# Output gate of the attention branch: a factor on the rows of the output weights, or a factor on the finished sums

## The chip, the cores and the metric

The kernel runs on one core of one Trainium2 chip. The metric is the device time of one launch in microseconds (us). The engines are named as the profile names them: PE (matrix multiply), PEld (its weight loads), DVE (VectorE), ACT (ScalarE), POOL (GpSimd) and SP (the queue that issues most DMAs). A difference of 0.3 % of this kernel's time is 3.5 us.

## The reference

One transformer block on x of shape (1, 1024, 1024), in float32: a normalisation, an input projection, two mixers side by side (a gated linear recurrence, and differential attention with 4 heads), one output projection for both, and a mixture of 16 experts. The lines that matter here:

```python
mix = jnp.dot(jnp.concatenate([y_lru, y_att], axis=-1), w_out[l])
x = x + gate1 * mix
h2 = rms_norm(x, g_norm2[l]) * (1.0 + scale2) + shift2
x = x + gate2 * expert_choice_ffn(h2, w_router[l], w1[l], w3[l], w2[l])
```

`gate1`, `scale2`, `shift2` and `gate2` are rows of 1024 numbers, one for each output column, worked out earlier from the input c. Since `gate1` scales columns of the result, it may as well scale the columns of `w_out`.

## The kernel before, in words

The program has five stages: projections and recurrence (0 to about 313 us in the trace), the attention loop (to 467), the output projection with residual, norm and router (to 575), the choice of tokens (to about 610), and the experts (to the end).

**Attention loop.** 32 steps, one for each head and tile of 128 query rows, are pipelined over `g`. In each step PE forms scores (`sc`), DVE adds the bias and finds the maximum (L768), ACT takes exponentials (`p`), DVE combines the two softmaxes (L807), PE transposes the weights (`pw`, L814), ACT copies them out (`wt`) and PE multiplies with the values (`pv`, 16 matmuls a step). Every fourth step a finished sum is evacuated: ACT copies `pv` to `o` (`o_evac`), POOL squares it in two pieces (`osq`, L837), and two steps later DVE reduces the squares over a row (`hov`, L845, first instruction of `o_rstd`), a short chain on DVE and POOL makes the inverse root (L846 to L858), POOL scales `o` (L861), and PE transposes it (`po`, L869) for `yatt`. PE, DVE and ACT run in the order in which the code was written (`manual_schedule`, L907). POOL and SP are outside that list and are put in order by the scheduler. All engines work through their own instructions strictly in order.

**Weights for the next stage.** `load_wo(k)` is called in eight of the loop's steps. It loads 128 rows of `w_out` (`wo`, L877), multiplies them on POOL by `gate1` in four pieces of 256 columns (L886), lets ACT round them to the high part (`who`, `wx0o` or `wos` by k), and lets POOL form the low part as a difference, again in four pieces (`wlo`, `wx1o`, `wos`, L890). The row `gate1` is spread over all partitions by one DMA before the loop (L906).

**Output projection.** For each of 8 tiles of 128 tokens: ACT and POOL (DVE in the first two tiles) split `y` into `yh` and `yl` (L1015). PE adds up 24 matmuls for each half of 512 columns (`mix`). `add_x` (L1040) lets DVE add the residual `xr` to the sums, half by half, the result over `xr`. ACT squares it into `tmp` (name `h2` in the code) with a row sum. PE transposes it (`ph`, L1059), ACT copies it (`x1T`), and PE multiplies with the router weights (`pl`, `pk`), from which DVE and ACT make the affinities (`afd`, L1098) and PE turns them (`pq`, L1101). After the next tile's first `add_x`, DVE makes `tmp = x1 * rs * na` (L1109), POOL adds `shift2` to all 1024 columns at once (L1110), and a DMA stores `tmp` as row tile of `h2d`, from which the experts gather later. The last tile takes its columns as 512, 256 and 256 (`mix7b`, `mix7c`), and forms the product on POOL (L1052). All engines but POOL and SP are ordered by the scheduler by estimated times here, too.

Of the kernel before, what the change touches and what calls it, by code (L numbers as in the profile page):

```python
# [8 lines left out]
F32 = mybir.dt.float32  # L9
F32R = mybir.dt.float32r  # L10
BF16 = mybir.dt.bfloat16
I32 = mybir.dt.int32
AF = mybir.ActivationFunctionType
ALU = mybir.AluOpType
# [4 lines left out]
P = 128  # L19
# [3 lines left out]
NT = S // P  # L23
NCT = 4
NH = 4
NE = 16
# [14 lines left out]
OA = (5, 6, 7)  # L41
NL0 = 16
NL1 = 30
XO = ("yh0", "yl0", "xr2", "xr0", "yh1", "yl1", "tmp0", "xr1", "na2", "shift2", "tmp1")
KG = 3
KA = 3
PI = 3
# [35 lines left out]
def tile_block(ctx: ExitStack, tc, x, cols, w_mod, b_mod, w_in, wa, wx, lam_qk, relT, w_out, g2, w_router,  # L83
               w1, w3, w2, jbits, jfrac, out):
    nc = tc.nc
    V, A, G_, T, SY = nc.vector, nc.scalar, nc.gpsimd, nc.tensor, nc.sync
# [29 lines left out]
    modd = [dram.tile([1, 2048], F32, name=f"modd{i}") for i in range(2)]  # L116
# [174 lines left out]
    mps, pms = {}, {}  # L291
# [583 lines left out]
    def load_wo(k):  # L875
        r = raw_tile(f"wo{k}", [P, D])
        SY.dma_start(out=r, in_=w_out[k * P:(k + 1) * P, :])  # L877
        if k < 3:
            woh[k], wol[k] = (wo1.tile([P, D], F32R, tag=tg, bufs=b_, name=f"{tg}o{k}") for tg, b_ in (("wh", NWH), ("wl", 3)))
        elif k == 3:  # L880
            woh[k], wol[k] = (wo1.tile([P, D], F32R, tag=f"wx{j}", bufs=1, name=f"wx{j}o") for j in range(2))
        else:
            woh[k], wol[k] = qk_tile(f"wos{k}", F32R)
        for q in range(4):
            qs = slice(q * 256, q * 256 + 256)
            G_.tensor_tensor(out=r[:, qs], in0=r[:, qs], in1=gate1[:, qs], op=ALU.mult)  # L886
        act(woh[k], r)
        for q in range(4):
            qs = slice(q * 256, q * 256 + 256)
            G_.tensor_tensor(out=wol[k][:, qs], in0=r[:, qs], in1=woh[k][:, qs].bitcast(F32), op=ALU.subtract)  # L890
# [10 lines left out]
    for k in range(NCT):  # L901
        G_.tensor_copy(y0[:, 0, k, :], y_lru[k][:, 0:P])
        G_.tensor_tensor(out=y0[:, 1, k, :], in0=y_lru[k][:, 0:P], in1=y0[:, 0, k, :].bitcast(F32), op=ALU.subtract)
    gate1 = ap.tile([P, 1024], F32, name="gate1")
    src = modd[0][:, 0:1024]
    SY.dma_start(out=gate1, in_=bass.AP(tensor=src.tensor, offset=src.offset, ap=[[0, P], [1, 1024]]))  # L906
    with tc.manual_schedule(engines={mybir.EngineType.PE, mybir.EngineType.DVE, mybir.EngineType.Activation}):  # L907
        for g in range(NG + 2):
            hn, u = divmod(g, 8)
# [64 lines left out]
    def row_bc(name, src):  # L974
        t_ = x_big(name, 0)
        SY.dma_start(out=t_, in_=bass.AP(tensor=src.tensor, offset=src.offset, ap=[[0, P], [1, 1024]]))
        return t_
# [7 lines left out]
    wrA = xt_["wrA"]  # L985
    G_.memset(wrA, 0.0)
    G_.tensor_tensor(out=wrA[:, :, 0:NE], in0=wr2, in1=a2c.unsqueeze(2).to_broadcast([P, KT, NE]), op=ALU.mult)
    shift2 = row_bc("shift2", modd[0][:, 1024:2048])
    na2 = row_bc("na2", modd[1][:, 0:1024])
    g2r = row_bc("tmp1", g2)  # L990
# [28 lines left out]
    for t in range(NT):  # L1019
# [7 lines left out]
        x1 = xr  # L1027
# [9 lines left out]

        def add_x(n):
            ns = slice(cuts[n] * P, cuts[n + 1] * P)
            add = V.tensor_tensor(out=x1[:, ns], in0=pms[n], in1=xr[:, ns], op=ALU.add)  # L1040
            if n == 0 and h2_pend:
                h2_pend.pop()(add)
            if n == 1 and t == NT - 1:
                with tc.issue_after(add.ins):
                    V.tensor_scalar(out=x_big("yh0", NT).bitcast(BF16)[:, 0:SE], in0=aTh[:, 0:SE], scalar1=jb.bitcast(F32),
                                    scalar2=None, op0=ALU.is_ge, op1=ALU.add, accum_out=cnt7)
            if t == 0 and n == 0:
                o_out(7)
            act(h2[:, ns] if t < NT - 1 else junk_[:, 0:(cuts[n + 1] - cuts[n]) * P], x1[:, ns], AF.Square, scale=1.0 / 32,
                accum_out=ssq2[:, t, n:n + 1])  # L1050
            if t == NT - 1:
                G_.tensor_tensor(out=h2[:, ns], in0=x1[:, ns], in1=na2[:, ns], op=ALU.mult)  # L1052
# [53 lines left out]
        if t < NT - 1:  # L1106
            def h2_fin(add, t=t, x1=x1, h2=h2):
                with tc.issue_after(add.ins):
                    V.scalar_tensor_tensor(out=h2, in0=x1, scalar=rs2[:, t:t + 1], in1=na2, op0=ALU.mult, op1=ALU.mult)  # L1109
                G_.tensor_tensor(out=h2, in0=shift2, in1=h2, op=ALU.add)  # L1110
                (G_ if t in HG else SY).dma_start(out=h2d[t * P:(t + 1) * P, :], in_=h2)

            h2_pend.append(h2_fin)
        else:
            with tc.issue_after(i_exp.ins):
                act(h2, h2, AF.Copy, scale=rs2[:, t:t + 1])
            i_h2 = G_.tensor_tensor(out=h2, in0=shift2, in1=h2, op=ALU.add)
            A.dma_start(out=h2d[sl, :], in_=h2)
# [31 lines left out]
        return lambda: V.tensor_scalar(out=o, in0=a, scalar1=b, scalar2=c, op0=ALU.mult, op1=ALU.add)  # L1150

    NR = 5
    rhs = late.tile([P, NT, NE, NR], BF16, name="rhs")
    tidx = late.tile([P, 56], F32, name="tidx")[:, 0:NT]
    pidx = late.tile([P, 1], F32, name="pidx")
    G_.iota(tidx, pattern=[[P, NT]], base=0, channel_multiplier=0, allow_small_or_imprecise_dtypes=True)
    G_.iota(pidx, pattern=[[0, 1]], base=0, channel_multiplier=1, allow_small_or_imprecise_dtypes=True)
    G_.tensor_copy(rhs[:, :, :, 0], tidx.unsqueeze(2).to_broadcast([P, NT, NE]))
# [8 lines left out]
    G_.tensor_copy(selb, bone.rearrange("p (e j) -> p e j", j=8)[:, :, 0])  # L1167
    idx = const.tile([P, NE], I32, name="idx")
    gat = const.tile([P, NE], F32, name="gat")
    slot = late.tile([P, NE, NT], F32, name="slot")  # L1170
    gth = []

    def pick(e, oh, pi):
# [290 lines left out]
```

## Time and profile before

| | |
|---|---|
| median of 3 runs | 1180.84 us (1180.72 to 1183.39) |
| the profiled execution itself | 1183.49 us |
| its span in the trace | 1181.8 us |
| mean granted clock of PE | 0.977 |
| PE busy | 1116.1 us (94 %) |
| DVE, ACT, POOL busy | 955.8, 791.3, 481.7 us |

The profiled execution is 2.65 us (0.22 %) above the median of the other runs, and its span is 1.7 us shorter than its own time. In rows of the timeline the columns are: start, duration, engine, line, operation, tiles, count, and in brackets the idle time ahead of it with what ended it. A row for one line lists minimum, median and maximum of one instruction in ns. A row for a stretch lists its bounds, its length, busy time of PE, PEld, DVE, ACT and POOL (with counts), the granted clock, the share of the DMA engines and GB/s.

### The profile page before, as it was taken

The numbers are of one execution on the slowest core, as the hardware profiler recorded it, in microseconds if no ns is written. First come the engines' busy times: TensorE is split into PE (matmuls) and PEld (weight loads), VectorE is DVE, ScalarE is ACT, GpSimd is POOL, SyncE is SP. The second block draws the span as 40 slices with busy tenths as digits, with TensorE's granted clock in tenths as the row PEclk, the third lists the DMA queues.
The fourth block names the chain that finished last, engine by engine and source line by source line (L and its number), as shares of the span: only waits on it lengthen the run. The fifth ranks groups of instructions, "written<-read, shape, count | busy, mean of one in ns | idle before, by whom it ended". The sixth has DMA issues, their size and how long they took to land.

```text
span 1181.8 us, 17872 instructions
## 1 busy us (share of the span) xinstructions
PE 1116.1 (94%) x6320; PEld 937.7 (79%) x6320; DVE 955.8 (81%) x1242; ACT 791.3 (67%) x1046; POOL 481.7 (41%) x540
## 2 busy tenths in 40 slices
PE   6999899999979999999569999999999999999996
PEld 4698898798869899777447888888888888888885
DVE  6897657875569896543679999999999999999995
ACT  7548282295467787543328887878888787888784
POOL 4693132133086646344534324444323444332400
PEclk9999999999999999999769999999999999999999
DMA  9765625704781505425799999999999999999911
GB/s 334 228 198 177 220 84 170 242 18 112 193 242 45 150 19 180 162 107 211 266 342 330 363 386 380 390 391 402 378 394 393 369 392 410 394 394 386 393 37 18
DMA packets 146994, 304.34 MB, mean 258 GB/s; under 512 B 16973, under 2 KB 43725, under 8 KB 146901
## 3 DMA queue, kind: packets, MB, share of 16 engines
q1 hardware_dynamic: 135008, 279.99, 65.7%
q0 software_dynamic: 5488, 19.45, 6.4%
q10 hardware_dynamic: 6408, 3.77, 1.1%
q8 instruction: 50, 0.82, 0.3%
q14 instruction: 40, 0.32, 0.1%
HBM read 277.95 MB, written 25.21 MB: 257 GB/s over the span
## 4 chain that ended last, share of the span: by engine, by line
PE 75%; DVE 7%; issue 5%; POOL 5%; DMA 5%; ACT 2%; SPq 1%; POOLq 0%; ACTq 0%; DVEq 0%
PE ab L93 28%; PE y L93 13%; PE mix L93 7%; PE pjz L93 4%; PE pjk L93 3%; PE sc L93 3%; PE pjv L93 3%; PE pv L93 3%; PE pw L814 2%; DMA wr<-in_w_mod_dram 2%; POOL wo L886 2%; PE pg L93 1%; DVE macc L623 1%; DMA wo<-in_w_out_dram 1%; PE pf L1348 1%
## 5 line engine op out<-in xcount | busy, mean ns | idle before, releaser
L1248 POOL TENSOR_SCALAR oh<-iot,slot 128x128 bf16<-128x128 bf16 x120 | 146.4, 1234 | 252.5 <-PE pf L1348 252.4
L93 PE MATMUL ab<-wh,xeh 128*128 128x512 f32 x512 | 202.2, 395 | 0.2 <-ACT xeh L90 0.2
L93 PE MATMUL ab<-wh,xel 128*128 128x512 f32 x512 | 199.7, 390 | 0.0
L93 PE MATMUL ab<-wl,xeh 128*128 128x512 f32 x512 | 157.7, 389 | 0.0
L93 PEld LDWEIGHTS ab<-wl,xeh 128*128 128x128 f32 x512 | 96.1, 188 | 20.4
L93 PEld LDWEIGHTS ab<-wh,xel 128*128 128x128 f32 x512 | 96.2, 188 | 19.5 <-DVE xel L1261 0.5
L93 PEld LDWEIGHTS ab<-wh,xeh 128*128 128x128 f32 x512 | 96.1, 188 | 19.5 <-ACT xeh L90 0.5
L141 DVE TENSOR_TENSOR wl<-w_0r,wh 128x1024 fp32r<-128x1024 f32 x79 | 96.8, 1226 | 10.2 <-ACT wh L90 0.4
L90 ACT ACTIVATE wh<-w_0r 128x1024 fp32r<-128x1024 f32 x81 | 86.1, 1062 | 24.8 <-PE ab L93 14.9
L141 DVE TENSOR_TENSOR wl<-w_3r,wh 128x1024 fp32r<-128x1024 f32 x79 | 96.7, 1225 | 6.2
L90 ACT ACTIVATE wh<-w_1r 128x1024 fp32r<-128x1024 f32 x79 | 83.5, 1058 | 23.7 <-PE ab L93 18.9
L90 ACT ACTIVATE wh<-w_3r 128x1024 fp32r<-128x1024 f32 x79 | 83.9, 1062 | 22.0 <-PE ab L93 17.4
L141 DVE TENSOR_TENSOR wl<-w_2r,wh 128x1024 fp32r<-128x1024 f32 x80 | 96.4, 1221 | 2.6 <-ACT wh L90 1.4
L90 ACT ACTIVATE wh<-w_2r 128x1024 fp32r<-128x1024 f32 x80 | 84.7, 1060 | 19.1 <-PE ab L93 18.7
L141 DVE TENSOR_TENSOR wl<-w_1r,wh 128x1024 fp32r<-128x1024 f32 x78 | 92.7, 1220 | 3.9 <-ACT wh L90 2.1
L768 DVE CUSTOM_DVE_ANT_0 p<-sc,bias 128x1024 f32<-128x1024 f32 x64 | 77.7, 1216 | 10.0 <-PE sc L93 9.9
L93 PE MATMUL y<-wh,htl 128*128 128x512 f32 x256 | 82.9, 395 | 0.0
L93 PE MATMUL y<-wh,hth 128*128 128x512 f32 x256 | 80.9, 396 | 0.0
L93 PE MATMUL y<-wl,hth 128*128 128x512 f32 x256 | 79.6, 391 | 0.0
L90 ACT ACTIVATE p<-p,stat 128x1024 f32<-128x1024 f32 x60 | 68.5, 1151 | 9.1 <-DVE stat L768 9.1
L93 PEld LDWEIGHTS pv<-v,wt 128*128 128x128 f32 x512 | 61.7, 192 | 2.5
L93 PE MATMUL pv<-v,wt 128*128 128x128 f32 x512 | 62.1, 275 | 0.0
(459 smaller groups left out, 2862.5 us busy)
## 6 DMA issues: line engine op xcount, KB each, us to landing
w_0r<-in_w_dram SPq DMA_DIRECT2D x81, 512.0 KB, 8.8
w_1r<-in_w_dram SPq DMA_DIRECT2D x79, 512.0 KB, 8.3
w_2r<-in_w_dram SPq DMA_DIRECT2D x78, 512.0 KB, 8.8
w_3r<-in_w_dram SPq DMA_DIRECT2D x77, 512.0 KB, 8.9
wr<-in_w_mod_dram SPq DMA_DIRECT2D x32, 512.0 KB, 4.9
wi<-in_w_in_dram SPq DMA_DIRECT2D x18, 512.0 KB, 4.4
w_5r<-in_w_dram SPq DMA_DIRECT2D x17, 512.0 KB, 8.0
wm<-in_w_mod_dram SPq DMA_DIRECT2D x32, 256.0 KB, 4.8
```

Source lines behind the costliest of these rows:

```text
L90: return A.activation(out=out, in_=in_, func=func, **kw)
L93: return T.matmul(out, lhsT=lhsT, rhs=rhs, start=start, stop=stop)
L141: return (eng or V).tensor_tensor(out=lo, in0=src, in1=hi.bitcast(F32), op=ALU.subtract)
L623: V.scalar_tensor_tensor(out=macc[i], in0=w, scalar=sc[:, k:k + 1], in1=macc[i], op0=ALU.mult, op1=ALU.add)
L768: V.tensor_tensor_reduce(out=p_, in0=scp[g, j], in1=prs[h][0][:, b0:b0 + S], op0=ALU.add, op1=ALU.min, scale=1.0, scalar=3.0e38, accum_out ...
L814: T.transpose(pw[:, b * P:(b + 1) * P], pt_[g, 0][:, kt * P:(kt + 1) * P], ident)
L886: G_.tensor_tensor(out=r[:, qs], in0=r[:, qs], in1=gate1[:, qs], op=ALU.mult)
L1248: G_.tensor_scalar(out=oh[:, t, :], in0=iot, scalar1=slot[:, e, t:t + 1], scalar2=None, op0=ALU.is_equal)
L1348: T.transpose(pt[:, b * P:(b + 1) * P], sa[:, b * P:(b + 1) * P], ident)
```

## The change

The weights are no longer multiplied by `gate1`; the sums are. In `load_wo` the four products of each call are left out, and ACT and POOL split the plain rows. In `add_x`, DVE first multiplies the sums in PSUM by `gate1` into `tmp` and then adds `xr` in a second instruction, whose inputs both lie in SBUF. The row `gate1` is loaded at the start of the output projection, ahead of `shift2`. POOL's addition of `shift2` is cut into four pieces of 256 columns (tiles 0 to 6). Four small tiles (`rhs`, `tidx`, `pidx`, `slot`) move to another pool, which opens after the output projection.

```diff
-XO = ("yh0", "yl0", "xr2", "xr0", "yh1", "yl1", "tmp0", "xr1", "na2", "shift2", "tmp1")
+XO = ("gate1", "yh0", "yl0", "xr2", "xr0", "yh1", "yl1", "tmp0", "xr1", "na2", "shift2", "tmp1")
...
-        for q in range(4):
-            qs = slice(q * 256, q * 256 + 256)
-            G_.tensor_tensor(out=r[:, qs], in0=r[:, qs], in1=gate1[:, qs], op=ALU.mult)
         act(woh[k], r)
...
-    gate1 = ap.tile([P, 1024], F32, name="gate1")
-    src = modd[0][:, 0:1024]
-    SY.dma_start(out=gate1, in_=bass.AP(tensor=src.tensor, offset=src.offset, ap=[[0, P], [1, 1024]]))
...
+    gate1 = row_bc("gate1", modd[0][:, 0:1024])
     shift2 = row_bc("shift2", modd[0][:, 1024:2048])
...
-            add = V.tensor_tensor(out=x1[:, ns], in0=pms[n], in1=xr[:, ns], op=ALU.add)
+            V.tensor_tensor(out=h2[:, ns], in0=pms[n], in1=gate1[:, ns], op=ALU.mult)
+            add = V.tensor_tensor(out=x1[:, ns], in0=h2[:, ns], in1=xr[:, ns], op=ALU.add)
...
-                G_.tensor_tensor(out=h2, in0=shift2, in1=h2, op=ALU.add)
+                for q in range(4):
+                    qs = slice(q * 256, q * 256 + 256)
+                    G_.tensor_tensor(out=h2[:, qs], in0=shift2[:, qs], in1=h2[:, qs], op=ALU.add)
...
-    rhs = late.tile([P, NT, NE, NR], BF16, name="rhs")
-    tidx = late.tile([P, 56], F32, name="tidx")[:, 0:NT]
-    pidx = late.tile([P, 1], F32, name="pidx")
+    rhs = moe.tile([P, NT, NE, NR], BF16, name="rhs")
+    tidx = moe.tile([P, 56], F32, name="tidx")[:, 0:NT]
+    pidx = moe.tile([P, 1], F32, name="pidx")
...
-    slot = late.tile([P, NE, NT], F32, name="slot")
+    slot = moe.tile([P, NE, NT], F32, name="slot")
```

In the changed file the lines up to L886 keep their numbers; behind it L890 becomes L887, L1040 becomes L1035 and L1036, L1059 becomes L1055, L1098 becomes L1094, L1109 becomes L1105, and L1110 becomes L1108.

On POOL at the start of the attention loop, behind the copies of the recurrence's first tile (`y`), there stood before:

```order
L903 TENSOR_TENSOR y_3005<-ylru_2727,y_3005 128x128
L886 TENSOR_TENSOR wo_3164<-wo_3164,gate_3014 128x256 x4
L886 TENSOR_TENSOR wo_3385<-wo_3385,gate_3014 128x256 x2
L890 TENSOR_TENSOR wlo_3167<-wo_3164,who_3166 128x256 x4
L886 TENSOR_TENSOR wo_3385<-wo_3385,gate_3014 128x256 x2
L886 TENSOR_TENSOR wo_3593<-wo_3593,gate_3014 128x256 x4
L886 TENSOR_TENSOR wo_3820<-wo_3820,gate_3014 128x256 x4
L886 TENSOR_TENSOR wo_4222<-wo_4222,gate_3014 128x256 x4
L886 TENSOR_TENSOR wo_4315<-wo_4315,gate_3014 128x256 x4
L837 TENSOR_TENSOR osq_3258<-o_3257 128x256 x2
L855 TENSOR_TENSOR hot_3340<-hoy_3341 128x4
```

And after the change, at the same place:

```order
L900 TENSOR_TENSOR y_3005<-ylru_2727,y_3005 128x128
L1124 MEMSET lsc 128x256
L1125 MEMSET lsc 128x32
L887 TENSOR_TENSOR wlo_3165<-wo_3162,who_3164 128x256 x4
L837 TENSOR_TENSOR osq_3252<-o_3251 128x256 x2
L855 TENSOR_TENSOR hot_3334<-hoy_3335 128x4
```

Eighteen products of five later weight tiles that stood between `wlo` of the first tile and the first `osq` are gone, and six ahead of `wlo`; the two short fills of `lsc` have come forward from the next stage. The two other groups of L886, each of four, stood further down, one of them directly ahead of the third `osq`; they are gone as well.

On DVE in the output projection, in the middle of the tiles (tile 3 being finished, tile 2's norm applied), there stood before:

```order
L1098 SCALAR_TENSOR_TENSOR afd<-pk_5056,lmx,lgm 128x128
L1040 TENSOR_TENSOR xr_3_5088<-mix_5091,xr_3_5088 128x512
L1109 SCALAR_TENSOR_TENSOR tmp_2_4967<-xr_0_4705,rs_4725,na_0_4711 128x1024
L1040 TENSOR_TENSOR xr_3_5088<-mix_5091,xr_3_5088 128x512
L1073 TENSOR_SCALAR ssq_4724<-ssq_4724 128x1
```

And after the change:

```order
L1035 TENSOR_TENSOR tmp_3_5070<-mix_5071,gate_0_4669 128x512
L1094 SCALAR_TENSOR_TENSOR afd<-pk_5036,lmx,lgm 128x128
L1036 TENSOR_TENSOR xr_3_5068<-tmp_3_5070,xr_3_5068 128x512
L1105 SCALAR_TENSOR_TENSOR tmp_2_4942<-xr_0_4672,rs_4693,na_0_4678 128x1024
L1035 TENSOR_TENSOR tmp_3_5070<-mix_5071,gate_0_4669 128x512
L1036 TENSOR_TENSOR xr_3_5068<-tmp_3_5070,xr_3_5068 128x512
L1069 TENSOR_SCALAR ssq_4692<-ssq_4692 128x1
```

Each half has a product ahead of its sum, and in the first half the affinities `afd` of the tile before now stand between the two.

On PE at the end of the same tile's second half (`mix_5091` before, `mix_5071` after; the next tile's first half is `mix_5214`, or `mix_5199`), there stood before:

```order
L93 MATMUL mix_5091<-wos_4538,yl_3_5071 128x512
L93 MATMUL pl_5169<-x1T,wrA 32x128 x4
L93 MATMUL mix_5214<-wlo_3388,yh_4_5193 128x512
L93 MATMUL mix_5214<-who_3387,yl_4_5194 128x512
L93 MATMUL mix_5214<-who_3595,yh_4_5193 128x512
L1059 MATMUL ph_1_5153<-ident,xr_3_5088 128x128 x4
L93 MATMUL mix_5214<-wlo_3596,yh_4_5193 128x512
```

And after the change:

```order
L93 MATMUL mix_5071<-wos_4508,yl_3_5051 128x512
L93 MATMUL pl_5154<-x1T,wrA 32x128 x4
L93 MATMUL mix_5199<-wlo_3382,yh_4_5178 128x512
L93 MATMUL mix_5199<-who_3381,yl_4_5179 128x512
L93 MATMUL mix_5199<-who_3585,yh_4_5178 128x512
L93 MATMUL mix_5199<-wlo_3586,yh_4_5178 128x512
L93 MATMUL mix_5199<-who_3585,yl_4_5179 128x512
L93 MATMUL mix_5199<-wx0o,yh_4_5178 128x512
L1055 MATMUL ph_1_5138<-ident,xr_3_5068 128x128 x4
L93 MATMUL mix_5199<-wx1o,yh_4_5178 128x512
```

The transposes `ph_1`, which wait for DVE's sum, stand behind six matmuls of the next tile where there were three; those of the first half have moved back by as much or more.

## The prediction

> **What bounds the kernel now.** I read the page first, then a table by stretches, and followed the chain of waits only where PE was not busy, since PE carries most of the time.
>
> ```profile
> PE 1116.1 (94%) x6320; PEld 937.7 (79%) x6320; DVE 955.8 (81%) x1242; ACT 791.3 (67%) x1046; POOL 481.7 (41%) x540
> ```
>
> The busy time of PE within the stretches that the change touches (its columns: bounds, length, PE, PEld, DVE, ACT, POOL, granted clock, DMA):
>
> ```profile
> 340.00:345.00 5.00, 5.00 (x39) 4.60 (x38) 3.08 (x4) 3.61 (x7) 5.00 (x7) 1.00 1.03 224
> 345.00:353.00 8.00, 1.12 (x10) 0.93 (x9) 2.41 (x8) 0.21 (x2) 6.24 (x13) 0.82 1.04 244
> 353.00:358.00 5.00, 4.97 (x19) 4.21 (x20) 4.93 (x9) 3.94 (x6) 4.30 (x11) 0.60 0.26 108
> 358.00:467.00 109.00, 108.53 (x783) 98.84 (x783) 96.18 (x186) 88.25 (x156) 65.91 (x128) 1.00 0.31 89
> 467.00:575.00 108.00, 108.00 (x631) 84.90 (x630) 48.72 (x152) 46.96 (x159) 40.61 (x60) 1.00 0.47 170
> ```
>
> Two things stand here. The attention loop is bound by PE, but for one hole of 8 us at 345, after which PE's granted clock is 0.60 for a while. And the output projection (467 to 575) has no hole at all: 108.00 of 108.00. So the removed work is worth something only at the hole, and the added work costs something only where it makes a hole in the last row. The chain of waits tells who made the hole:
>
> ```profile
> 320.59 11.15 DMA wo<-in_w_out_dram
> ...
> 334.96 4.40 POOL wo L886 x5
> 339.36 9.95 POOL wo L886 x13
> 349.31 1.15 POOL osq L837 x2
> 350.48 0.69 DVE hov L845
> 351.84 1.12 DVE p L768
> 353.03 2.07 PE sc L93 x4
> ...
> 384.67 3.80 POOL wo L886 x4
> 388.47 1.16 POOL osq L837 x2
> 389.65 0.69 DVE hov L845
> ```
>
> POOL multiplied five weight tiles that nobody needed yet, and the squares `osq` stood behind them. DVE's reduction `hov` needs `osq`, and behind `hov` in DVE's order stands the next L768, which frees the score buffer that PE wants. At 384.67 the same happens with a single group.
>
> **What the removed products give.** The length of the hole is read from PE's own period, the start of `pv` in successive steps:
>
> ```profile
> 339.65 1.95 PE L93 MATMUL pv<-v,wt 128*128 128x128 f32 x16
> 344.17 1.95 PE L93 MATMUL pv<-v,wt 128*128 128x128 f32 x16
> 353.03 1.22 PE L93 MATMUL sc<-kh,qs 128*128 128x512 f32 x2 [6.91 <-DVE stat L768]
> ...
> 357.73 1.95 PE L93 MATMUL pv<-v,wt 128*128 128x128 f32 x16
> 390.19 1.95 PE L93 MATMUL pv<-v,wt 128*128 128x128 f32 x16
> 395.88 1.95 PE L93 MATMUL pv<-v,wt 128*128 128x128 f32 x16
> ```
>
> An undisturbed step takes 344.17 - 339.65 = 4.52 us. The step with the hole takes 357.73 - 344.17 = 13.56 us, so it costs 9.04: 6.91 of waiting, and the rest from matmuls at the clock of 0.60 and from refilling the pipeline. The second takes 395.88 - 390.19 = 5.69, which costs 1.17. Together 10.21 us.
>
> Does all of it go? What is late next must be asked of the same chain without L886:
>
> ```profile
> 329.84 1.06 ACT L90 ACTIVATE who<-wo 128x1024 fp32r<-128x1024 f32 x1 [1.80 <-POOL wo L886]
> 337.25 0.60 ACT L90 ACTIVATE o<-pv 128x512 f32<-128x512 f32 x1
> 342.93 0.15 DVE L798 RECIPROCAL stat<-s_sum 128x1 f32<-128x1 f32 x1
> L837 POOL TENSOR_TENSOR osq<-o x14: 606/613/615, 349.3 to 463.8; 128x256 f32<-128x256 f32 x14
> L890 POOL TENSOR_TENSOR wlo<-wo,who x12: 723/736/1722, 332.1 to 379.6; 128x256 fp32r<-128x256 f32 x12
> ```
>
> ACT is ready for `who` 1.80 us earlier, at 328.04, and done by about 329.1. POOL's four `wlo` pieces (4 x 0.74) end by about 332.1. `o` is there at 337.85, two `osq` pieces take 1.23, so `osq` is done at about 339.1. DVE reaches `hov` only after L798, at 343.08: 4 us to spare. I take the whole 10.21, and for the lower end of the gain I suppose that something else on POOL takes up to 4 of it (the first rival).
>
> **What the added work costs.** Three rows give the new durations, and two show what POOL and DVE do to one another:
>
> ```profile
> L1040 DVE TENSOR_TENSOR xr<-mix,xr x15: 683/692/692, 480.7 to 569.0; 128x512 f32<-128x512 f32 x15
> L1015 POOL TENSOR_TENSOR yl<-yatt,yh x24: 453/460/463, 489.1 to 552.6; 128x128 fp32r<-128x128 f32 x24
> L1110 POOL TENSOR_TENSOR tmp<-shift,tmp x7: 2383/2394/2400, 492.8 to 572.1; 128x1024 f32<-128x1024 f32 x7
> L886 POOL TENSOR_TENSOR wo<-wo,gate x32: 720/730/1723, 327.0 to 387.7; 128x256 f32<-128x256 f32 x32
> L807 DVE SCALAR_TENSOR_TENSOR p<-p,stat,p x30: 1284/1286/1878, 321.7 to 464.2; 128x1024 f32<-128x1024 f32 x30
> ```
>
> The product has the shape and the sources of L1040 (PSUM and SBUF), so 0.69 us. The new sum reads two SBUF tiles, and no DVE row of just that shape stands in this stage; I take 0.69 for it as well. 15 halves and two quarters add 15 x 0.69 + 2 x 0.42 = 11.2 us to DVE, which is busy for 48.72 of 108: room enough, and only the place counts.
>
> *Middle tiles.* These are the rows of one tile:
>
> ```profile
> 509.14 0.69 DVE L1040 TENSOR_TENSOR xr<-mix,xr 128x512 f32<-128x512 f32 x1 [5.01 <-PE mix L93]
> 510.19 0.60 PE L1059 MATMUL ph<-ident,xr 128*128 128x128 f32 x4
> 515.66 0.40 PE L93 MATMUL mix<-wlo,yh 128*128 128x512 f32 x1
> 515.89 0.39 PE L93 MATMUL mix<-who,yl 128*128 128x512 f32 x1
> ```
>
> `ph` began 1.05 us after DVE's sum began. Successive matmuls start 0.23 apart (515.66, 515.89), and the new order puts three more ahead of `ph`, so `ph` wants the sum at 510.19 + 0.69 = 510.88. DVE delivers it at 509.14 + 0.69 + 0.69 = 510.52. That leaves 0.36 us. In the first half four more stand ahead of `ph` (0.92), against 0.69 more on DVE and at most the short `afd`. So PE has no hole here unless the sum itself is slowed, and the last two rows above say that it may be. L807 reads two SBUF tiles on DVE; its median is 1.286 us, and its longest, 1.878, lies beside L886, whose own longest is 1.723 instead of 0.730. The second half's sum will lie beside POOL's `yl` pieces of 0.46. If it waits for one of them to end, it is late by 0 to 0.46, of which 0.36 is covered. I take 0.1 in each of 6 tiles, 0.6 us, with 0 and 2.8 (0.46 in each) as its ends.
>
> The Trainium skill ("SBUF — State Buffer", section "Who interferes with whom") says that a DVE instruction with two SBUF inputs and a GpSimd instruction that reads SBUF exclude each other through the whole of an instruction. The two longest values above agree, while the medians show that most instances escape. By the rule alone every sum that meets a POOL instruction would wait for its end, which makes the third rival.
>
> *First tiles.* Here DVE makes product, sum and the norm row one after another:
>
> ```profile
> 479.55 1.23 DVE L991 SCALAR_TENSOR_TENSOR na<-na,tmp 128x1024 f32<-128x1024 f32 x1
> gate<-modd SPq DMA_DIRECT2D x1, 512.0 KB, 4.8
> ```
>
> L991 now stands between the second product of tile 0 and its two sums, and tile 1's product behind those. Its path to PE grows by between 0 and 1.23 + 0.69 = 1.92 us; I take 1.2, since there is neither a spare tile of sums nor other work for PE. The row `gate1` itself is fetched some 13 us before the first product could run (the loop's last L807 ends near 465.5, the first product follows at about 479), and took 4.8 us to land, so I cost it at nothing. If that were gone, the stage would start later by what the row is late.
>
> *Last tile.*
>
> ```profile
> 575.44 0.42 DVE L1040 TENSOR_TENSOR xr<-mix7c,xr 128x256 f32<-128x256 f32 x1 [1.48 <-PE mix7c L93]
> 605.34 1.07 POOL L1180 DMA_INDIRECT xe<-h2d,idx  x1 [12.84 <-DVE idx L1177]
> ```
>
> Behind the last quarter PE has nothing else, so its product lies on the path in full: 0.42. The sum behind it may meet a POOL piece of 256 columns, 0 to 0.73 (L886's median); I take half of it, together 0.8.
>
> *POOL.* Four pieces take 4 x 0.73 = 2.92 instead of 2.39, in a stage in which POOL is busy for 40.61 of 108. The index tiles filled after the last tile instead of before the first fall into the 12.84 us in which POOL waits for DVE. Both cost nothing; were that cover gone, the price would be 0.5 in each of 7 tiles, and less than the 12.84.
>
> **The sum.** -10.21 + 0.6 + 1.2 + 0.8 = -7.6 us. The profiled execution (1183.49) would become 1175.9; it lies 2.65 above the median of the runs, a difference that the change does not touch, so from the median: 1180.84 - 7.6 = 1173.2 us. About 0.3 %, 3.5 us, is what a measurement of this kernel can tell from no change.
>
> **The rivals.**
>
> 1. *Part of the hole stays.* POOL's `wlo` group and `osq` (4 x 0.74 + 1.23 = 4.2 us) come late together, because the weight tile lands late: the chain began with `wo` coming off DMA. Against it stands the time to spare of 4 us. It would give back about 4: 1177.2. Chance 0.10.
>
> 2. *Slower: the gate step becomes the bound of the output projection.* Place: `ph` in both halves of all 8 tiles. Price: product 0.69 and a blocked sum 0.46, 1.15 a half, if the matmuls put ahead of `ph` do not cover them, for instance because these wait in turn for `yl`, which POOL makes and which the sums would hold up. 16 x 1.15 = 18.4, and with 1.2 and 0.42 against 10.21: +9.8, 1190.6. It turns slower by over 3.5 us once a half loses (10.21 + 3.5 - 1.6) / 16 = 0.76 us. For it speaks that PE has no idle time there to lose, against it that DVE has half of the stage free and `yl` is made a tile ahead. Chance 0.06.
>
> 3. *Every new sum is blocked by POOL for one piece.* 15 sums by 0.46 and two by 0.73 make 8.4 in place of my 0.6 and of half a piece, uncovered: -10.21 + 0.42 + 1.2 + 8.4 = -0.2, 1180.6. Against it: the sum of a first half falls where POOL had been idle. This is what the Trainium skill ("SBUF — State Buffer", section "Who interferes with whom") would have if all lay on the path. Chance 0.07.
>
> 4. *The hole has another cause*, and the loop waits as long for something else, such as the keys of the next head (the DMA engines are full through it, at 1.04). Then only the costs remain: 1180.84 + 2.6 = 1183.4. Against it: DVE's wait ends with `osq` to the tenth of a microsecond. Chance 0.04.
>
> **How the numbers follow.** My forecast has 0.71; its own range is 1170.6 (no cost but the last product) to 1176.5 (the upper ends 2.8, 1.92 and 1.15 of the costs, with the gain whole: -10.21 + 5.87 = -4.3). A gain beyond it has 0.02. Faster by over 3.5 us (below 1177.3) are the forecast, what lies beyond it, and the first rival at its price: 0.83. Same are rivals 3 and 4: 0.11. Slower is rival 2: 0.06. For 8 in 10 the range must hold the forecast and the first rival; to its lower end I add the 0.47 of idle time that PE has left in the loop and 1.1 for the spread of runs, to its upper end the first rival with the costs a little above their middle: 1169.0 to 1179.5.
>
> **What would show it.** Right: no L886 on POOL, `osq` done ahead of DVE's L798, steps of 4.52 us from the first to the last of the loop with the clock at 1.00, so that the loop ends about 10 us earlier; PE idle for 1 to 3 us in the output projection, mostly in the first two tiles; the last sum of the last tile 0.4 to 1.2 later behind its matmuls. Wrong: another wait of several us on `hov` in the loop; or `ph` waiting for DVE in every tile, by more than 0.76 a half; or sums of 512 columns that take 1.1 us or more instead of 0.69.

## The result, and the profile after

| | before | after |
|---|---|---|
| median of 4 runs each, same chip | 1181.49 us (1180.72 to 1183.39) | 1173.2 us (1172.1 to 1173.91) |
| ratio to before, 95 % interval | 1 | 0.9927 (0.9909 to 0.9944) |
| the profiled execution itself | 1183.49 us | 1173.91 us |
| its span | 1181.8 us | 1171.2 us |

The changed kernel is 0.73 % faster, 8.3 us between the medians. The forecast was 1173.2.

The busy time of the engines, from the page of the changed kernel:

```profile
PE 1112.2 (95%) x6319; PEld 933.9 (80%) x6320; DVE 967.1 (83%) x1259; ACT 791.4 (68%) x1046; POOL 462.5 (39%) x529
```

DVE is 11.3 us busier (955.8 before), against the 11.2 reckoned. POOL has lost 19.2 us. The stretches of the loop and of the output projection, from the table by stretches (bounds, length, PE, PEld, DVE, ACT, POOL, granted clock, DMA):

```profile
320.00:345.00 25.00, 25.00 (x180) 22.82 (x179) 23.10 (x45) 20.11 (x36) 8.32 (x18) 1.00 0.84 246
345.00:360.00 15.00, 15.00 (x107) 13.68 (x106) 13.40 (x27) 12.11 (x23) 6.64 (x12) 1.00 0.49 139
360.00:457.00 97.00, 97.00 (x700) 88.74 (x699) 84.31 (x163) 80.05 (x140) 52.77 (x106) 1.00 0.37 104
457.00:565.00 108.00, 107.67 (x630) 82.33 (x628) 60.85 (x170) 44.69 (x156) 47.30 (x79) 1.00 0.48 170
```

The hole is gone: PE is busy for 15.00 of 15.00 where it had been busy for 1.12 of 8.00, and the granted clock is 1.00 throughout where rows of 0.82 and 0.60 stood. The last row has 0.33 us of idle PE that was not there; the prediction had named 1 to 3 us of it as a sign of being right, and this sign did not come. Waits of PE in this stage sit inside rows that count as busy; one is shown below, at 517.28. The steps of the loop at the two places of the old holes, from the timeline of PE:

```profile
341.55 1.95 PE L93 MATMUL pv<-v,wt 128*128 128x128 f32 x16
346.06 1.95 PE L93 MATMUL pv<-v,wt 128*128 128x128 f32 x16
...
378.50 1.95 PE L93 MATMUL pv<-v,wt 128*128 128x128 f32 x16
383.01 1.95 PE L93 MATMUL pv<-v,wt 128*128 128x128 f32 x16
```

Both steps are 4.51 us long, where 13.56 and 5.69 had stood. Why, POOL's timeline and DVE's tell:

```profile
326.73 3.80 POOL L887 TENSOR_TENSOR wlo<-wo,who 128x256 fp32r<-128x256 f32 x4 [14.14 <-ACT who L90]
335.29 1.19 POOL L837 TENSOR_TENSOR osq<-o 128x256 f32<-128x256 f32 x2 [4.75 <-ACT o L90]
```

```profile
339.25 0.16 DVE L798 RECIPROCAL stat<-s_sum 128x1 f32<-128x1 f32 x1
339.33 0.67 DVE L845 TENSOR_REDUCE hov<-osq 128x4 f32<-128x512 f32 x1
```

`osq` is done at 336.48, 2.85 us ahead of DVE's `hov` at 339.33, which has no bracket: it waits for nothing. (The forecast had 4 us to spare; counted from the mark used below, DVE comes to `hov` 1.4 us earlier than in the trace of before, where its L807 takes 1.68 and 1.88 us beside the products instead of 1.29. Half of the products are already enough to use the slack up, as b_half shows.) Of DVE's waits for `osq` in the loop one is left, late in it; it stands in the trace of before as well:

```profile
DVE hov L845 <- POOL osq L837: 0.6, 1, 0.6
```

**Where the time went, stage by stage.** The traced executions differ by some 2 us ahead of the loop in which nothing was changed, so all stages are counted from a mark shortly ahead of the loop: the start of PE's third run of `pjv` matmuls (287.06 in the trace of before, 284.73 in that of its repetition). The other marks are PE's first `mix`, DVE's first instruction on `mix7c`, PE's last `pq`, and POOL's first gather of `xe`; in us, worked out from the starts in each timeline:

| kernel | loop, to first `mix` | to `mix7c` | to last `pq` | to first gather | sum |
|---|---|---|---|---|---|
| before | 180.32 | 108.06 | 5.31 | 24.59 | 318.28 |
| before, repeated (b_copy) | 180.67 | 108.18 | 5.31 | 24.61 | 318.77 |
| b_nogate | 169.78 | 108.04 | 5.31 | 24.60 | 307.72 |
| b_half | 171.06 | 108.11 | 5.31 | 24.60 | 309.08 |
| b_order | 175.17 | 108.10 | 5.32 | 24.59 | 313.18 |
| b_order2 | 170.14 | 108.06 | 5.31 | 24.60 | 308.10 |
| b_order2r | 170.20 | 108.11 | 5.32 | 24.59 | 308.22 |
| **after** | **169.82** | **109.63** | **5.76** | **25.43** | **310.64** |
| after, repeated (a_copy) | 169.90 | 109.65 | 5.77 | 25.45 | 310.77 |
| a_noprod | 169.81 | 108.09 | 5.31 | 25.44 | 308.65 |
| a_psum | 169.79 | 109.68 | 5.77 | 25.43 | 310.67 |
| a_onepiece | 169.75 | 109.63 | 6.80 | 25.44 | 311.62 |
| a_cut | 169.75 | 109.62 | 5.76 | 24.94 | 310.07 |

From before to after: loop -10.50, output projection +1.57, its tail +0.45, threshold search +0.84; together -7.64. The last column but one holds the surprise.

### The profile page after: what moved, and what is told of

Read it like the earlier page. It is cut to its first block, busy times and chain, and to the rows that moved or that the text cites. A ratio compares the mean times of both kernels' runs of the same rounds, so it can differ in the third digit from the quotient of the medians.

```text
span 1171.2 us, 17874 instructions
## 1 busy us (share of the span) xinstructions
PE 1112.2 (95%) x6319; PEld 933.9 (80%) x6320; DVE 967.1 (83%) x1259; ACT 791.4 (68%) x1046; POOL 462.5 (39%) x529
## 4 chain that ended last, share of the span: by engine, by line
PE 79%; DVE 8%; DMA 4%; issue 4%; ACT 2%; POOL 2%; POOLq 0%; ACTq 0%; DVEq 0%
PE ab L93 28%; PE y L93 13%; PE mix L93 7%; PE pv L93 5%; PE sc L93 5%; PE pjk L93 3%; PE pjv L93 3%; PE pjz L93 3%; DMA wr<-in_w_mod_dram 2%; PE pw L814 2%; DVE macc L623 2%; PE pg L93 1%; PE pf L1346 1%; PE pe L1255 1%; DVE junk L1133 1%
```

## The experiments

Theory A, that of the prediction: the hole comes from the order of POOL's queue, the squares `osq` standing behind products that nobody needs yet. Its rival, theory B: it comes from the amount of POOL work beside the loop, whatever its order. The first four kernels below shared a chip (before: 1181.66 us, 11 runs), the next four another (1182.11, 11 runs), the last three a third series (1182.0, 11 runs); so they are compared by their ratios to before, and directly only within a series.

**Before, repeated (b_copy).** No edit.

> The kernel before, unchanged, profiled a second time, to see what of the difference between the two traces lies ahead of the attention loop and belongs to no edit (before and after reach the first value projection, pjv, at 287.1 and 284.7 us). If that is a spread of executions, this trace has its pjv anywhere between 284 and 288, while the step with the hole (start of pv to start of the next pv, 13.56 us) repeats within 0.3 us, and the second (5.69) too. If it belongs to the change, pjv stands at 287.1 again.

It took 1181.47 us in its one execution. Its long steps are 13.92 and 5.72 us, 9.40 and 1.20 more than 4.52 (before: 9.04 and 1.17). The first is 0.36 longer than in the first trace, a little more than the 0.3 allowed for. The holes belong to the kernel and not to one execution, and a stage is good to some 0.4 us.

**Before without the products (b_nogate).**

```diff
-        for q in range(4):
-            qs = slice(q * 256, q * 256 + 256)
-            G_.tensor_tensor(out=r[:, qs], in0=r[:, qs], in1=gate1[:, qs], op=ALU.mult)
         act(woh[k], r)
```

> The kernel before without the products on the weights, and with no gate in their place (gate1 is left out of the result). Theory A (the hole comes from osq standing behind L886 on POOL): steps of 4.52 us all through the loop, the output projection as before with PE at 108.0 of 108; 10.2 to 10.5 us faster than before, about 1171.1. It is then faster than the changed kernel by what the gate costs there: by the two traces 1.4 in the output projection, 0.45 at its end and 0.85 in the search for the threshold, so about 2 to 2.7 us. Theory B (the gain is in proportion to POOL's work): the same here.

1170.85 us, ratio 0.9912 (0.9897 to 0.9926). The loop is as short as that of the changed kernel (169.78, against 169.82). So the whole of the loop's gain is the products' removal, and what the changed kernel pays elsewhere shows as the difference of the two: 307.72 against 310.64, 2.92 us.

**Before with half of the products (b_half).**

```diff
-        for q in range(4):
+        for q in range(2):
```

> The kernel before with half of the products: two of four pieces (the gate is left out for half of the columns). Theory A: the ten pieces that remain ahead of the first osq end near 340 and osq near 341, before DVE wants it at 343.1, so the hole is gone whole: 9.5 to 10.5 us faster than before, within 1 us of the kernel without products. Theory B, in which the loop pays for the work itself (POOL's share, or its hold on the memory port): half of the gain, 4 to 6 us faster.

1171.97 us, ratio 0.9922 (0.991 to 0.9935). DVE's waits for `osq` in the loop:

```profile
DVE hov L845 <- POOL osq L837: 1.8, 2, 1.3
```

Half of the products leave 1.28 of the loop's 10.5 us, not half: one step of 5.67 us. The expectation, that nothing of the hole stays, was missed by this step: `osq` came 1.26 us after DVE was ready for it, since the ten products left ahead of it took 8.97 us and not 10 x 0.73, and `wlo` ahead of them 3.81 and not 2.82. That is still theory A, where the loss starts only once the queue ahead of `osq` is longer than its slack. B would have left about 5.

**All products, each issued behind the newest square (b_order).** Nothing is left out; only POOL's order differs from before.

```diff
+    last_sq = []
...
-            (V if n == 7 else G_).tensor_tensor(out=sq[:, i], in0=o[:, i], in1=o[:, i], op=ALU.mult)
+            last_sq.append((V if n == 7 else G_).tensor_tensor(out=sq[:, i], in0=o[:, i], in1=o[:, i], op=ALU.mult))
...
-            G_.tensor_tensor(out=r[:, qs], in0=r[:, qs], in1=gate1[:, qs], op=ALU.mult)
+            with tc.issue_after(*([last_sq[-1].ins] if last_sq else [])) if last_sq else ExitStack():
+                G_.tensor_tensor(out=r[:, qs], in0=r[:, qs], in1=gate1[:, qs], op=ALU.mult)
```

> The kernel before with all 32 products on the weights, but each ordered behind the newest osq that is written in the code ahead of it, so that no osq stands behind products of later weight tiles. The result is whole. Theory A: the hole and the smaller one are gone, nothing is added elsewhere: 8.5 to 10.5 us faster than before, 1171 to 1173, as fast as the changed kernel or up to 2.5 us faster. Theory B: as much POOL work as before, so no change (1181).

1177.04 us, ratio 0.9958 (0.9945 to 0.9971): slower than expected. The early holes are gone (steps of 4.52), but late in the loop two others stand, steps of 5.88 and 8.84 us. At the second, POOL's timeline has

```profile
432.92 5.55 POOL L889 TENSOR_TENSOR wo<-wo,gate 128x256 f32<-128x256 f32 x8
438.41 1.19 POOL L857 TENSOR_TENSOR hot<-hoy 128x4 f32<-128x4 f32 x1
```

and DVE's timeline beside it the short chain behind `hov`:

```profile
433.59 0.78 DVE L848 SCALAR_TENSOR_TENSOR hot<-s_sum 128x4 f32<-128x4 f32 x1
434.39 0.66 DVE L849 SCALAR_TENSOR_TENSOR hov<-hov,hot 128x4 f32<-128x4 f32 x1
435.08 0.66 DVE L854 TENSOR_SCALAR hoy<-hov 128x4 int32<-128x4 int32 x1
435.78 0.65 DVE L855 TENSOR_SCALAR hoy<-hoy 128x4 int32<-128x4 int32 x1
```

In the changed kernel, with POOL idle at that place, the same four read

```profile
433.26 0.15 DVE L846 SCALAR_TENSOR_TENSOR hot<-s_sum 128x4 f32<-128x4 f32 x1
433.45 0.16 DVE L847 SCALAR_TENSOR_TENSOR hov<-hov,hot 128x4 f32<-128x4 f32 x1
433.64 0.17 DVE L852 TENSOR_SCALAR hoy<-hov 128x4 int32<-128x4 int32 x1
433.85 0.17 DVE L853 TENSOR_SCALAR hoy<-hoy 128x4 int32<-128x4 int32 x1
```

Each of the four takes about as long as one product (5.55 / 8 = 0.69) and starts 0.7 behind the one before: each waits out one POOL piece. And POOL's own half of the chain (L857) stands behind all eight. So the order matters twice: products may not stand ahead of the squares, and not between a square and the chain that follows it either.

**All products, behind the chain (b_order2).** As b_order, but the products of the third and later tiles are issued after POOL has scaled an earlier `o` (L861), that is, behind its chain; the first two tiles' products stay ahead of the first square. The whole result is computed.

```diff
+    o_sc = {}
+    AN = {2: 0, 3: 1, 4: 2, 5: 3, 6: 3, 7: 4}
...
-            (V if h == NH - 1 else G_).tensor_tensor(out=o[:, i], in0=o[:, i], in1=yb, op=ALU.mult)
+            o_sc[n] = (V if h == NH - 1 else G_).tensor_tensor(out=o[:, i], in0=o[:, i], in1=yb, op=ALU.mult)
...
-            G_.tensor_tensor(out=r[:, qs], in0=r[:, qs], in1=gate1[:, qs], op=ALU.mult)
+            with tc.issue_after(o_sc[AN[k]].ins) if k in AN else ExitStack():
+                G_.tensor_tensor(out=r[:, qs], in0=r[:, qs], in1=gate1[:, qs], op=ALU.mult)
```

> The kernel before with all products on the weights, at other places on POOL: the first two weight tiles' ahead of the first osq, and each further one behind a scaling of o (L861 before), where POOL waits for the next osq and DVE has no short instructions. The result is whole. Theory A refined (POOL's products cost only where osq stands behind them, or where DVE's short chain behind hov lies beside them): no hole in the loop, and an output projection as before: 1170.5 to 1172, 1 to 2.5 us faster than the changed kernel. If the amount of POOL work counts by itself, at least what the first reordering lost stays: 1176 to 1178.

1172.29 us, ratio 0.9918 (0.9899 to 0.9938), on the second chip. The longest step of the loop is 5.12 us, and the loop takes 170.14: all 32 products are done, in another order, and the 10 us are gained nonetheless. Theory B falls with this run.

**The changed kernel without the product (a_noprod).**

```diff
-            V.tensor_tensor(out=h2[:, ns], in0=pms[n], in1=gate1[:, ns], op=ALU.mult)
-            add = V.tensor_tensor(out=x1[:, ns], in0=h2[:, ns], in1=xr[:, ns], op=ALU.add)
+            add = V.tensor_tensor(out=x1[:, ns], in0=pms[n], in1=xr[:, ns], op=ALU.add)
```

> The changed kernel with add_x as before: the sums are read from PSUM and xr is added in one instruction, and no gate is applied anywhere (gate1 is left out of the result). It prices the added instruction with all that follows from it. By the two traces the gate step costs 0.5 in the first tiles, 0.9 in the middle ones (0.23 in each of four) and 0.45 behind the last sum, so 1.6 to 2.2 us less than the changed kernel: 1171.0 to 1171.6, and the middle tiles are 13.34 us apart instead of 13.57. If the middle tiles stay at 13.57, the loss there does not come from the product.

1171.12 us, ratio 0.9905 (0.9888 to 0.9923). Output projection and tail are back at 108.09 and 5.31: the second DVE instruction costs 1.54 + 0.45 = 2.0 us. But the threshold search stays at 25.44, so its +0.84 has nothing to do with the product.

**The product left in PSUM (a_psum).** The sum reads PSUM and `xr` instead of two SBUF tiles.

```diff
-            V.tensor_tensor(out=h2[:, ns], in0=pms[n], in1=gate1[:, ns], op=ALU.mult)
-            add = V.tensor_tensor(out=x1[:, ns], in0=h2[:, ns], in1=xr[:, ns], op=ALU.add)
+            V.tensor_tensor(out=pms[n], in0=pms[n], in1=gate1[:, ns], op=ALU.mult)
+            add = V.tensor_tensor(out=x1[:, ns], in0=pms[n], in1=xr[:, ns], op=ALU.add)
```

> The changed kernel with the product written back to PSUM instead of into tmp, so that the sum has one SBUF input again; the result is whole. Two theories for the 0.23 us in the middle tiles. Theory R: PE waits for the product, since the second half of a tile may only begin when DVE has read the first half; the sums are now held for the sum as well, but the written order puts eight matmuls and four transposes in between (four before), which covers it, so tiles are 13.34 apart and 0.9 us are won: about 1172.3. Theory S: PE is late because the sum, with two SBUF inputs, is held up by POOL: the same gain here, but then the longest sum (0.95 in the changed kernel) must fall to 0.69, and PE's wait must have been in front of the transposes. Both are told apart by the trace: in R the waits on the product vanish, in S those on the sum. If holding the sums longer costs more than the order covers: 2 to 4 us slower than the changed kernel.

1173.76 us, ratio 0.9927 (0.991 to 0.9944): no difference from the changed kernel that can be measured. The sums, from the rows of the tile `xr`, and a row of PE's timeline in the first tiles:

```profile
L1036 DVE TENSOR_TENSOR xr<-mix,xr x15: 678/691/692, 473.3 to 559.7; 128x512 f32<-128x512 f32 x15
```

```profile
474.05 0.66 PE L1055 MATMUL ph<-ident,xr 128*128 128x128 f32 x4 [1.38 <-DVE xr L1036]
```

No sum is held by POOL any more (longest 0.692 us, against 0.947), and a middle tile takes 13.36 us; but the first tiles take that back, with a wait of 1.38: at the first half of the third tile this kernel is 1.51 us behind b_nogate, the changed one 0.46. So the 0.9 us expected were not won. The two theories for the middle tiles part at the waits: between 484 and 545 us no wait of PE's `mix` for DVE is left here, where the changed kernel has five, 1.7 us in all. That speaks for theory R; the rows are shown below, with the middle tiles.

**The shift in one piece (a_onepiece).**

```diff
-                for q in range(4):
-                    qs = slice(q * 256, q * 256 + 256)
-                    G_.tensor_tensor(out=h2[:, qs], in0=shift2[:, qs], in1=h2[:, qs], op=ALU.add)
+                G_.tensor_tensor(out=h2, in0=shift2, in1=h2, op=ALU.add)
```

> The changed kernel with the shift added in one instruction of 1024 columns, as before. In the middle tiles no sum falls beside it, so nothing changes there. In the last tile the sum of the second part (at 561.4 in the trace) falls beside it and would wait for up to 2 us, of which the next part's matmuls cover most: 0 to 1.5 us slower than the changed kernel. If the pieces matter in every tile (theory S for all sums): 5 us slower or more.

1175.22 us, ratio 0.9942 (0.9923 to 0.9962). The timeline of DVE and POOL at the last quarter:

```profile
562.02 2.63 POOL L1106 TENSOR_TENSOR tmp<-shift,tmp 128x1024 f32<-128x1024 f32 x1
...
565.17 1.46 DVE L1036 TENSOR_TENSOR xr<-tmp,xr 128x256 f32<-128x256 f32 x1
565.60 0.74 POOL L1048 TENSOR_TENSOR tmp<-xr,na 128x256 f32<-128x256 f32 x1
```

The last sum takes 1.46 us instead of 0.42, and the tail 6.80 instead of 5.76: the four pieces save 1.04 us of the tail. The sum that the expectation had in view, that of the part before, was not held (0.42, at 561.97; the long piece began only at 562.02). The long piece itself is over by 564.65; the sum is not beside it but beside POOL's issue of a DMA (564.95 to 565.58) and the piece of L1048 that was pushed back to 565.60, and its end at 566.63 lies 0.29 behind the end of that piece. That the sum is held and the tail longer by the same amount is shown; which instruction holds it is not settled by these rows.

**POOL's weight pieces cut beside the threshold search (a_cut).** This one asks for the cause of the +0.84. The pieces in question are POOL's subtractions for the first expert's weights (`wl`), cut from one of 1024 columns to four of 256.

```diff
+        if eng is G_:
+            act(hi, r)
+            for q in range(4):
+                qs = slice(q * 256, q * 256 + 256)
+                G_.tensor_tensor(out=lo_[:, qs], in0=r[:, qs], in1=hi[:, qs].bitcast(F32), op=ALU.subtract)
+            return hi, lo_
```

> The changed kernel with POOL's three subtractions for the first expert's weights, which lie beside the threshold search, cut from one piece of 1024 columns to four of 256; all else as it was. Theory L (DVE's instruction of 128 x 7 is held until the POOL instruction then running has ended): the 128 x 7 instruction ends together with the end of a POOL piece, so that it takes between 0.29 and some 0.9 us instead of 1.14, and the way from the last pq to the first gather of xe is 0 to 0.85 us shorter than in the changed kernel, about half of that in the middle. Rival M (POOL's order has made it slow in another way, or it is slow beside any POOL work): it stays at 1.1 us and does not end with a piece. The whole time is expected to differ by less than a measurement can tell under either.

In the changed kernel DVE's timeline has, in the threshold search,

```profile
575.96 1.14 DVE L1195 TENSOR_SCALAR misc<-misc 128x7 f32<-128x7 f32 x1
```

and POOL's beside it

```profile
572.43 4.64 POOL L141 TENSOR_TENSOR wl<-w_0r,wh 128x1024 fp32r<-128x1024 f32 x2
```

In the kernel before, the two were, on DVE and on POOL,

```profile
586.80 0.29 DVE L1197 TENSOR_SCALAR misc<-misc 128x7 f32<-128x7 f32 x1
```

```profile
584.72 2.34 POOL L141 TENSOR_TENSOR wl<-w_0r,wh 128x1024 fp32r<-128x1024 f32 x1
```

In both, DVE's instruction ends 0.03 us behind POOL's (577.10 and 577.07; 587.09 and 587.06). With the pieces cut, on DVE and on POOL:

```profile
576.13 0.63 DVE L1195 TENSOR_SCALAR misc<-misc 128x7 f32<-128x7 f32 x1
```

```profile
576.01 0.72 POOL L1320 TENSOR_TENSOR wl<-w_0r,wh 128x256 fp32r<-128x256 f32 x1
```

It ends at 576.76, again 0.03 behind the end of the piece (576.73), and is 0.51 us shorter, as is the way to the first gather (24.94 against 25.43 to 25.45). In each of the 13 traces this instruction ends 0.02 to 0.04 us behind the end of a POOL piece. Theory L is borne out: the instruction is held until POOL's is over. The time was 1172.68 us, ratio 0.9916 (0.9891 to 0.9941), within what the measurement can tell.

**The changed kernel and b_order2 side by side (a_copy, b_order2r).** No edits beyond those above.

> The changed kernel once more, unaltered, on the same chip as the two others, so that they can be compared with it directly. Expected: 0.993 of the kernel before, within its earlier interval (0.9909 to 0.9944), and in its trace the same three costs: 0.23 us in the middle tiles, last product 0.42, the instruction of 128 x 7 in the threshold search at 1.1 instead of 0.29 us.

> The kernel before, with the products left on the weights and moved behind the scaling of o in POOL's queue, a second time and on the same chip as the changed kernel. By the traces of the first time it saves what the changed kernel saves and has none of its three costs (1.63 us in the output projection with the tail's 0.45, and 0.85 in the threshold search), but keeps some 0.4 to 0.6 us in the loop: expected 1 to 2.5 us below the changed kernel. If the rival holds, that POOL's products among the squares cost as much as they save elsewhere, it is level with it.

1175.85 us (1173.95 to 1177.67), ratio 0.9948 (0.9928 to 0.9968), against 1170.59 us (1169.53 to 1172.03), ratio 0.9901 (0.9882 to 0.9921): neither the runs nor the intervals overlap. Keeping the products on the weights, in a better place of POOL's queue, beats both kernels. The stages explain 310.77 - 308.22 = 2.55 us of it, the upper end of the 1 to 2.5 expected; the medians differ by 5.3. The other 2.7 are in no stage of the two traces (the copy's profiled execution was its fastest, 1173.95), and a_copy's ratio lies just above the changed kernel's first interval, where it had been expected to fall; what made it slower in that series is left open.

## Why the prediction was right

The sum came out at -7.6 where the traces show -7.64. The mechanism of the gain was right; of the costs, one term is right by size alone, one was twice too large, and one that was put at nothing was not nothing.

- **The holes (-10.21):** -10.50 in the loop. The two long steps are gone whole; of the rest, 0.21 was in the step just ahead of the first hole (4.73 us, from 334.92 to 339.65 in the trace of before, against 4.52), which the forecast did not count. That the whole of it goes is shown by b_nogate, and that the cause is the order of the queue by b_half and b_order2. Rival 1 (part of the hole stays) and rival 4 (another cause) fell.
- **Middle tiles (0.6):** the size is right, the cause wrong. Three tile periods are 13.56 us instead of b_nogate's 13.34, together 0.66 (the forecast had spread its 0.6 over six tiles). The price was set on sums held by POOL's `yl` pieces. These do occur, from the rows of the instructions:

```profile
L1035 DVE TENSOR_TENSOR tmp<-mix,gate x15: 679/691/692, 466.1 to 557.6; 128x512 f32<-128x512 f32 x15
L1036 DVE TENSOR_TENSOR xr<-tmp,xr x17: 424/692/947, 471.9 to 564.6; 128x512 f32<-128x512 f32 x15, 128x256 f32<-128x256 f32 x2
L1010 POOL TENSOR_TENSOR yl<-ylru,yh x24: 453/462/1447, 470.5 to 539.5; 128x128 fp32r<-128x128 f32 x24
```

  Here is such a sum on DVE, and PE beside it:

```profile
511.13 0.92 DVE L1036 TENSOR_TENSOR xr<-tmp,xr 128x512 f32<-128x512 f32 x1
```

```profile
511.69 0.39 PE L93 MATMUL mix<-who,yl 128*128 128x512 f32 x1
511.92 0.40 PE L93 MATMUL mix<-wx0o,yh 128*128 128x512 f32 x1
512.15 0.61 PE L1055 MATMUL ph<-ident,xr 128*128 128x128 f32 x4
```

  The sum ends at 512.05, and `ph` begins at 512.15, the usual 0.23 behind the matmul ahead of it: the six matmuls cover the hold. What costs is another wait, one that the prediction did not look for. From the waits in the output projection:

```profile
PEld mix L93 <- DVE tmp L1035: 1.7, 5, 0.4
...
PEld ph L1055 <- DVE xr L1036: 1.5, 7, 0.2
...
PE ph L1055 <- DVE xr L1036: 0.5, 1, 0.5
```

  and in one tile, from the timeline at the end of its first half:

```profile
516.85 0.69 DVE L1035 TENSOR_TENSOR tmp<-mix,gate 128x512 f32<-128x512 f32 x1 [0.21 <-PE mix L93]
...
517.28 0.82 PE L93 MATMUL mix<-who,yh 128*128 128x512 f32 x2
517.60 0.19 PEld L93 LDWEIGHTS mix<-who,yh 128*128 128x128 f32 x1 [0.36 <-DVE tmp L1035]
```

  A tile's two halves are parts of one tile of sums (`mix`), and PE starts the second half only when the product has read the first. The second matmul of the row at 517.28 begins at about 517.71 (the row's end, 518.10, less 0.39 for one), 0.43 behind the first instead of 0.23. Four matmuls of the next tile stand in between, as before the change, but the `ph` transposes, which had filled the gap too, have moved behind it. Without the product (a_noprod) the wait is gone, and a middle tile takes 13.35; with more matmuls in between (a_psum) it is gone as well. So the step "`ph` wants the sum at 510.88, DVE delivers it at 510.52" was worked out for one reader of the half and not for its next writer.
- **First tiles (1.2):** 0.56 against b_nogate at DVE's first instruction on the second half of the third tile; the term was twice too large, within its bounds of 0 and 1.92. The order was as said: the norm row (L991, now L986, 1.32 us at 470.69) stands between the second product and the two sums. These take 1.82 together instead of 2 x 0.69, beside POOL's `yl`; how much of the 0.56 is due to that is not shown.
- **Last tile (0.8):** 0.45 behind `mix7c`, for which the 0.8 was reckoned; another 0.36 came just ahead of it, for which nothing was. From DVE's timeline of the last quarter:

```profile
564.15 0.42 DVE L1035 TENSOR_TENSOR tmp<-mix7c,gate 128x256 f32<-128x256 f32 x1 [1.12 <-PE mix7c L93]
564.61 0.42 DVE L1036 TENSOR_TENSOR xr<-tmp,xr 128x256 f32<-128x256 f32 x1
```

  The product lies on the path in full, as said, but the sum behind it is not held (0.42); the half of a POOL piece was not paid. What it is worth is seen in a_onepiece.
- **POOL ("both cost nothing"):** this failed, by 0.84 us, the largest single error. That POOL has 12.84 us of idle time (12.73 after) says that its work costs nothing by its length. But the fills that came later put two pieces of `wl` back to back, and so moved the end of the piece that holds DVE's 128 x 7 instruction: from 6.10 us behind the start of the last shift (587.06 - 580.96) to 6.95 (577.07 - 570.12), while DVE was ready at the same 5.84 in both. The two shifts' rows on POOL, of before and of after:

```profile
580.96 2.35 POOL L1117 TENSOR_TENSOR tmp<-shift,tmp 128x1024 f32<-128x1024 f32 x1 [4.08 <-ACT tmp L90]
```

```profile
570.12 2.35 POOL L1115 TENSOR_TENSOR tmp<-shift,tmp 128x1024 f32<-128x1024 f32 x1 [3.25 <-ACT tmp L90]
```

  All kernels made from the changed one with whole pieces have it, none made from the one before. That the four moved tiles alone do it is argued from that, not tried apart from the rest.
- **Rivals 2 and 3:** `ph` waits for DVE eight times and by at most 0.5 (before: five times, by at most 0.3), and 13.6 us is the longest middle tile; the gate step did not become the bound. Sums are held, but in the middle tiles under cover.
- **The range:** its lower end of 1170.6 for "no cost but the last product" leaves out that product too; with its 0.42 it is 1171.05.

Three errors nearly cancel: the loop gained 0.29 more than reckoned, output projection and tail cost 2.02 instead of 2.6, and the threshold search cost 0.84 that was put at nothing. And the forecast started from 1180.84, where the four runs of before have a median of 1181.49, so that the medians differ by 8.3 and not by 7.6. The agreement to a tenth is luck; the working itself was good to about 1 us.

## What to carry to other kernels

When a wait in an in-order queue costs time, ask first whether the work ahead of it can stand elsewhere in the queue: here the products in another place gained as much as taking them out, without their price on another engine. When an instruction is put between a matmul and its reader, follow the tile of sums to its next writer as well as to its next reader. And work on an engine with idle time is free by its length only: where its instructions hold another engine's, the place at which one of them ends is on the path.

## What the runs showed of the hardware

Some very short DVE instructions are held for the rest of a running POOL instruction: 128 x 4 ones at 0.65 to 0.78 instead of 0.15 to 0.17 us (b_order), the 128 x 7 one at 1.14, 0.63 and 0.29, each time ending 0.03 us behind POOL's. Those of a single column are not (0.15 us for the 128 x 1 one at 575.77, beside the same long POOL piece that held the 128 x 7 one), nor are reductions (`hov` 0.67 with POOL idle, 0.69 beside the products of b_order), nor products that read PSUM (at most 0.692). The Trainium skill ("SBUF — State Buffer", section "Who interferes with whom") says that the second to issue is blocked for the whole of the other's instruction, when DVE has two SBUF inputs while the other reads SBUF, or when DVE is in one of its two-port modes, which it says `tensor_scalar` can enter and `tensor_reduce` on this chip cannot. These rows agree, also for `tensor_scalar` on int32 and on as few as four columns. What had been weighed in the prediction was the length of such a hold on long instructions; on short ones it is a multiple of their own time.
